# First layer in a written order: scan parts at fixed distances, weight splits in pieces, products in two halves, and changed ends

## The chip, the cores and the metric

The kernel runs on one core of a Trainium2 chip. A core has a matrix engine (TensorE, PE in the profile; its weight loads are shown apart as PEld), a vector engine (VectorE, DVE), a scalar engine (ScalarE, ACT), a general engine (GpSimd, POOL), and an engine that starts transfers (SyncE, SP). Matmuls write to PSUM, which has eight banks of 128 rows by 512 numbers; everything else lies in SBUF. The metric is the device time of one execution in microseconds (us).

## The reference, cut to what matters

The input is x, 512 tokens by 1024 features, float32. There are two layers and a last norm.

```python
# layer 1: Mamba-2 (8 groups g, 4 heads each, head size 64, state 128)
h = rms_norm(x, norm_g)
z, xbc, dt = split(h @ w_in)                  # 2048 gates, 2048 + 2*1024 scan inputs, 32 steps
xs, bm, cm = silu(causal_conv4(xbc))
for each chunk:                               # the kernel takes chunks of 128 tokens
    cb     = cm @ bm.T                        # per group
    y_diag = (cb * decay) @ (xs * dt)         # per head
    y_off  = (cm @ state) * exp(acs)
    state  = state * exp(acs_end) + bm.T @ (xs * dt * to_end)
y = y_diag + y_off + d_skip * xs
u = y * silu(z);  u = u * rsqrt(mean_per_group(u*u) + eps)
x = x + (u * g) @ w_out
# layer 2: differential attention, 8 heads; k, v from rms_norm(x), q and gate from rms_norm(x)
w   = softmax(q1 @ k1.T - alibi) - lam * softmax(q2 @ k2.T - alibi)
x   = x + (rms_norm(w @ v) * silu(gate)) @ w_bo
out = rms_norm(x, final_norm_g)
```

## The kernel before, in words

**Three matmuls for one product.** Dense products keep float32 accuracy by splitting each operand into a head and a rest: head·head, head·rest, rest·head (`mm3`, line 225). These three matmuls of 128x512 are called a step here. Weights come by transfer as `raw` (128 x 2048 numbers a half item); ScalarE makes the heads (`whi`) and VectorE the rests (`wlo`), four operations of 128x512 each for every half item.

**The dense stream.** Layer 1 is a list of items (line 90, `order_a`): `z0 g0 g1 z1 g2 g3 z2 g4 o0 g5 z3 g6 g7 o1 o2 o3`. An item z projects gates of 512 columns for four token tiles, g projects the B, C and two x parts of one group (four banks `pg`), o is a part of the output projection. Each item has two halves of 16 steps. The evictions of a g item are the convolution and SiLU (`xc`), on VectorE and ScalarE, a bank after the other.

**The scan.** `ssd(g)` computes group g from its four `xc` outputs: `pcb` (C by B), `pbt` and `pxt` (transposes of B and of the two x parts), decays times `pcb` (`dec`, on VectorE, from exponentials on ScalarE that `decays` makes for two groups at once), `psA` and `psB` (states), `pyd` (the diagonal part: 16 products of 128x64, in two banks), `po` with `hst` (offsets by the states). Then on VectorE, GpSimd and ScalarE: `tmp` (offsets scaled), sums into `dx`, the gate `zs`, squares, a root by nine small VectorE operations (`rsqrt`, line 231), and the scaling to `tmp` on ScalarE. Last, `pyt` transposes `tmp`, and `yh`, `yl` are the head and rest that the o items read.

**What sets the order.** The program is written against a scheduler that sorts each engine's instructions by its own timeline. A switch per engine (`Ordered`, line 43, `T.on`, `A.on`, `V.on`) keeps an engine in the order of the program instead. Before, all three are off in layer 1 but for the first splits: `ssd(g)` is written when item g has been written, and the scheduler places its parts. In layer 2 TensorE is on for the whole layer: the dense stream is a generator that yields its length after each step, and `paced` lays due pieces of weight splits (`use_b`) beside it. In layer 1 `use` splits whole half items and fetches three half items ahead.

**The end.** The last head's last token tile is turned (`turn`), weighed with the values, normed and gated; beside it runs `rows`, the last output projection, in an order written by hand as (tile, half, heads). A finished half is added to the residual on VectorE (`add`), squared on ScalarE, and its tile's root (`last_root`) scales it on its way out.

Of the kernel before, what the change touches and what calls it, by code (L numbers as in the profile page):

```python
# [17 lines left out]
P = 128  # L18
# [43 lines left out]
def trunk(ctx, tc, x, x_t, par, w_dt, w_in, w_out, w_kvqg, w_bo, d_skip, lam_qk, fin_g, out):  # L62
# [59 lines left out]
    def load(i):  # L122
# [29 lines left out]
        if i == 0:  # L152
# [6 lines left out]
            nc.sync.dma_start(raw[:, 2:4, :].rearrange("p k n -> p (k n)"), src[:, 2 * w:4 * w])  # L159
            for i in range(1, 4):  # L160
                nc.sync.dma_start(xt[i], x_t[:, 2 * i:2 * i + 2, :])
# [15 lines left out]
    def use(seg):  # L177
        fetch(segs.index(seg) + 3)
        return ready.pop(seg)

# [15 lines left out]
    def use_b(seg, first=None, pace=None):  # L196
# [28 lines left out]
    def mm3(ps, lhs, rhs, first, last):  # L225
        (lh, ll), (rh, rl) = lhs, rhs
        T.matmul(ps, lhsT=lh, rhs=rh, start=first, stop=False)
        T.matmul(ps, lhsT=lh, rhs=rl, start=False, stop=False)
        T.matmul(ps, lhsT=ll, rhs=rh, start=False, stop=last)
# [44 lines left out]

    def fill(n):
        for _ in range(n):
            next(dense[0], None)
# [46 lines left out]
    def tok_mm(ps, t, b, w):  # L324
        tk = slice(t * P, (t + 1) * P)
        for k in range(4):
            kk = 4 * b + k
            mm3(ps, (hh[:, kk, tk], hl[:, kk, tk]), (w[0][:, k, :], w[1][:, k, :]), b == 0 and k == 0, b == 1 and k == 3)
            yield
# [27 lines left out]

    first = load(0)()
# [14 lines left out]
    fetch(2)  # L373
    for t in range(NT):
# [73 lines left out]
    ps_tt = ss_bank("ps_tt")  # L448
    for i, src in enumerate((dtp, acs, toe)):
        T.transpose(ps_tt[:, i * P:(i + 1) * P], src, ident)  # L450
    tok = const.tile([P, 4, NQ, H], F32, name="tok")
    V.tensor_copy(tok[:, 0:3].rearrange("p a c h -> p (a c h)"), ps_tt[:, 0:3 * P])
    A.activation(tok[:, 3], tok[:, 1], AF.Exp)
    dt_tok, acs_tok, toe_tok, eacs_tok = (tok[:, i] for i in range(4))

# [24 lines left out]
    def group_proj(g):  # L480
# [3 lines left out]
        for b in range(2):  # L484
            wh, wl = use(("g", g, b))
            for i in range(4):
                cs = slice(i * P, (i + 1) * P)
                for k in range(4):
# [3 lines left out]
                    yield  # L492
# [4 lines left out]
    def out_mm(po, j, t, w):  # L497
        tk = slice(t * P, (t + 1) * P)
        for k in range(4):
            yh, yl = yT[2 * j + k // 2]  # L500
            mm3(po, (yh[:, k % 2, tk], yl[:, k % 2, tk]), (w[0][:, k, :], w[1][:, k, :]), k == 0, k == 3)
            yield

    def out_proj(j):
        for n in range(2 if j < 3 else 1):
            w = (use if j < 3 else use_b)(("o", j, n))
# [9 lines left out]
    def stream_a():  # L516
# [4 lines left out]
        while True:  # L521
            yield

    bss = small.tile([P, 2, NT], F32, name="bss", bufs=1)
    decs = {}

    def decays(j):

        for g in (2 * j, 2 * j + 1):
            hs = slice(R * g, R * g + R)  # L530
            dec = bp.tile([P, R, NQ, P], F32, tag="dec", name=f"dec{g}", bufs=2)
            nc.sync.dma_start(dec.rearrange("p h c l -> p (h c l)"),
                                acs_d[hs].rearrange("h c l -> (h c l)").partition_broadcast(P))
# [13 lines left out]
    def ssd(g):  # L547
        bc, cc, x0, x1 = conv_out.pop(g)
# [4 lines left out]
        pcb = long_bank(f"pcb{g}")  # L553
        for c in range(NQ):
            cs = slice(c * P, (c + 1) * P)
            T.matmul(pcb[:, cs], lhsT=bc[:, cs], rhs=cc[:, cs], start=True, stop=True)
# [4 lines left out]
        A.copy(bt.rearrange("p c n -> p (c n)"), pbt[:, 0:3 * P])  # L561
        xdt = bp.tile([P, NQ, R, HD], F32, tag="xdt", name=f"xdt{g}")
# [15 lines left out]

        hst = bp.tile([P, 3, R, HD], F32, tag="hst", name=f"hst{g}")
# [6 lines left out]
        V.tensor_tensor(out=hsf[:, 1], in0=psA[:, 256:512], in1=hsf[:, 1], op=ALU.add)  # L586
        psB = ss_bank(f"psB{g}")
# [6 lines left out]
        pyd = []  # L594
        for q in range(2):
            pyd.append(ss_bank(f"pyd{g}_{q}"))
            for c in (2 * q, 2 * q + 1):
                for h in range(R):
                    o = (c % 2) * 256 + h * HD
                    T.matmul(pyd[q][:, o:o + HD], lhsT=dec[:, h, c, :], rhs=xdt[:, c, h, :], start=True, stop=True)  # L600
            dq = dx[:, 2 * q:2 * q + 2].rearrange("p c h e -> p c (h e)")
            V.tensor_tensor(out=dq, in0=pyd[q].rearrange("p (c e) -> p c e", c=2), in1=dq, op=ALU.add)
        if g % 2 and g < G - 1:
            decays((g + 1) // 2)

        po1 = ss_bank(f"po1{g}")
# [19 lines left out]
        for c in range(NQ):  # L626
            A.activation(tm[:, c], u[:, c], AF.Copy, scale=r4[:, c:c + 1])
# [454 lines left out]
```

## Time and profile before

| | |
|---|---|
| median of 3 runs | 739.06 us (738.97 to 739.16) |
| profiled execution | 739.31 us |
| its span in the trace | 737.5 us |
| TensorE busy | 723.7 us, 98% |
| VectorE, ScalarE, GpSimd busy | 532.8, 444.7, 115.7 us |
| layer 1, layer 2, tail after the last matmul | about 0 to 440, 440 to 728.5, 728.5 to 737.5 |

A row of the timeline has start, length, engine, line, operation, output<-inputs, shapes and count; in brackets what its engine waited for before. All operations of the three switched engines pass through one helper, so they show line 53 and are told apart by their tiles. Lengths of matmuls are modelled and overlap; the distance between two starts tells what one costs. Groups of instructions give busy time and the mean length of one.

### The profile page before, as it was taken

Reading aid. Unit: us, or ns where it says so; the run is one execution under the profiler, and the core shown is the slowest. Engines: PE = TensorE matmul, PEld = TensorE weight load, DVE = VectorE, ACT = ScalarE, POOL = GpSimd, SP = SyncE. Lnnn points to the kernel's source line nnn. Section 1 sums busy time; section 2 is a strip of 40 time slices with the busy share of each in tenths; the row PEclk is TensorE's granted clock in tenths of the full one; section 3 lists DMA queues with packets and bytes.
Section 4 is the critical chain, followed back from the end, with each engine's and each line's share of the span. In section 5 each row is a group of like instructions: output and inputs, shape, how many; then the busy total and the mean of one; then the engine's idle time right before and its main releaser. Section 6 shows DMA issues by size and latency. Waiting matters only on the chain.

```text
span 737.5 us, 10321 instructions
## 1 busy us (share of the span) xinstructions
PE 723.7 (98%) x3733; PEld 605.8 (82%) x3733; DVE 532.8 (72%) x1202; ACT 444.7 (60%) x974; POOL 115.7 (16%) x158
## 2 busy tenths in 40 slices
PE   9999999999999999999999999999999999999995
PEld 7788878888887888877888879888988898888874
DVE  5679955799668669469895755657767857785876
ACT  5849672865829356256433258767766766755565
POOL 0108141403233141150110201000000000000002
PEclk9999999999999999999999999999999999999998
DMA  8552313124131223132113220331221131131003
GB/s 315 212 194 95 118 55 115 63 109 172 58 114 61 112 114 115 58 115 101 71 58 114 94 79 8 114 115 58 73 100 57 59 115 58 58 105 68 28 1 114
DMA packets 12626, 70.83 MB, mean 96 GB/s; under 512 B 1696, under 2 KB 2464, under 8 KB 5024
## 3 DMA queue, kind: packets, MB, share of 16 engines
q1 hardware_dynamic: 12432, 70.16, 26.2%
q8 instruction: 29, 0.48, 0.3%
q14 instruction: 21, 0.17, 0.1%
q10 hardware_dynamic: 144, 0.02, 0.0%
HBM read 68.02 MB, written 2.16 MB: 95 GB/s over the span
## 4 chain that ended last, share of the span: by engine, by line
PE 85%; DVE 7%; ACT 5%; issue 1%; DMA 1%; POOL 0%; ACTq 0%; POOLq 0%; SPq 0%
PE pg L53 20%; PE po L53 13%; PE pz L53 10%; PE pt L53 7%; PE pq L53 6%; PE pv L53 6%; PE pk L53 6%; PE pyd L53 4%; PE pb L53 3%; PE sc L53 3%; PE pc L53 2%; DVE wlo L53 2%; ACT L53 1%; ACT whi L53 1%; PE pxt L53 1%
## 5 line engine op out<-in xcount | busy, mean ns | idle before, releaser
L53 DVE SCALAR_TENSOR_TENSOR wlo<-raw,prm,whi 128x512 fp32r<-128x512 f32 (+1 forms) x256 | 151.4, 639 | 50.1 <-ACT whi L53 49.8
L53 ACT ACTIVATE whi<-raw,prm 128x512 fp32r<-128x512 f32 (+1 forms) x256 | 136.8, 606 | 55.9 <-PE pz L53 12.9
L53 PE MATMUL pg<-a_hi,whi 128*128 128x512 f32 x256 | 102.4, 401 | 0.4 <-DVE xc L53 0.4
L53 PE MATMUL pg<-a_hi,wlo 128*128 128x512 f32 x256 | 102.7, 405 | 0.0
L53 PE MATMUL pg<-a_lo,whi 128*128 128x512 f32 x256 | 101.4, 397 | 0.0
L53 DVE SCALAR_TENSOR_TENSOR xc<-pg,prc,xc 128x511 f32<-128x511 f32 (+2 forms) x96 | 70.0, 741 | 4.6 <-ACT xc L53 3.8
L53 PEld LDWEIGHTS pg<-a_hi,whi 128*128 128x128 f32 x256 | 48.2, 188 | 11.4 <-issue 0.8
L53 PEld LDWEIGHTS pg<-a_lo,whi 128*128 128x128 f32 x256 | 48.2, 188 | 10.8
L53 PEld LDWEIGHTS pg<-a_hi,wlo 128*128 128x128 f32 x256 | 48.1, 188 | 10.9
L53 PE MATMUL po<-whi,yh 128*128 128x512 f32 x128 | 51.1, 401 | 0.6 <-ACT yh L53 0.6
L53 PE MATMUL po<-wlo,yh 128*128 128x512 f32 x128 | 51.0, 401 | 0.4 <-DVE wlo L53 0.4
L53 PE MATMUL pz<-wlo,a_hi 128*128 128x512 f32 x128 | 50.5, 401 | 0.0
L53 PE MATMUL po<-whi,yl 128*128 128x512 f32 x128 | 50.0, 397 | 0.0
L53 PE MATMUL pz<-whi,a_lo 128*128 128x512 f32 x128 | 49.9, 399 | 0.0
L53 ACT ACT_TABLE_LOAD x33 | 42.3, 1283 | 12.4 <-DVE xc L53 7.6
L53 PE MATMUL pz<-whi,a_hi 128*128 128x512 f32 x128 | 49.5, 399 | 0.2 <-ACT a_hi L53 0.2
L927 POOL TENSOR_TENSOR ot<-ot,fg 128x512 f32<-128x512 f32 x4 | 5.5, 1402 | 257.9 <-ACT ot L53 257.9
L53 ACT ACTIVATE s<-s,mx 128x128 f32<-128x128 f32 (+3 forms) x64 | 35.5, 557 | 9.5 <-DVE mx L53 9.2
L575 POOL TENSOR_TENSOR xe<-xdt,tok 128x256 f32<-128x256 f32 x24 | 15.4, 670 | 152.7 <-DVE xdt L53 152.7
L53 DVE CUSTOM_DVE_ANT_0 s<-sc,bias 128x128 f32<-128x128 f32 (+3 forms) x64 | 29.3, 487 | 12.3 <-PE sc L53 11.8
L53 PE MATMUL pv<-whi,b_hi 128*128 128x256 f32 x128 | 36.6, 286 | 0.0
L537 POOL TENSOR_TENSOR dec<-dec,tok 128x512 f32<-128x512 f32 x32 | 35.9, 1151 | 0.6
(240 smaller groups left out, 1728.7 us busy)
## 6 DMA issues: line engine op xcount, KB each, us to landing
raw<-in_w_in SPq DMA_DIRECT2D x23, 1024.0 KB, 4.8
raw<-in_w_kvqg SPq DMA_DIRECT2D x16, 1024.0 KB, 4.7
dec<-acs_d SPq DMA_DIRECT2D x8, 1024.0 KB, 5.1
raw<-in_w_out SPq DMA_DIRECT2D x8, 1024.0 KB, 4.7
raw<-in_w_bo SPq DMA_DIRECT2D x4, 1024.0 KB, 4.8
x_tok<-in_x SPq DMA_DIRECT2D x4, 512.0 KB, 10.4
out<-ot SPq DMA_DIRECT2D x8, 256.0 KB, 2.1
xt<-in_x_t SPq DMA_DIRECT2D x3, 512.0 KB, 7.8
```

The costliest lines, as they stand in the source:

```text
L53: i = op(*args, **kw)
L537: GP.tensor_tensor(out=dec[:, h], in0=dec[:, h], in1=acs_tok[:, :, R * g + h].unsqueeze(2).to_broadcast([P, NQ, P]), op=ALU.subtract)
L575: GP.tensor_tensor(out=xe[:, c], in0=xdt[:, c], in1=toe_tok[:, c, hs].unsqueeze(2).to_broadcast([P, R, HD]), op=ALU.mult)
L927: GP.tensor_tensor(out=o, in0=o, in1=f, op=ALU.mult)
```

## The change

It has six parts.

1. TensorE is on (in program order) for all of layer 1. `ssd(g)` becomes a generator that yields the number of dense steps until its next part. With `g` done, `pbt` comes after 4 steps, `pcb` at 5, `pxt` at 9 and 13, `psA` at 19, `psB` at 20, `pyd` at 21 and 25, `po` at 29, `pyt` at 45. VectorE, ScalarE and GpSimd stay with the scheduler.
2. The former `use_b` is used for all items: raw weights are fetched two half items ahead, their splits are written in four pieces beside the steps of the half item before.
3. The transfers of the decay rows are issued group by group behind `pyd` (`decay_rows`), and the rest of `decays` is written behind the norm of the odd groups.
4. Each 128x64 product of `pyd` is written as two of 64x64, for output rows 0 to 63 and 64 to 127.
5. At the start: an operation of ScalarE on the identity matrix comes first; two of the first transfers are split in two; group 0's first raw weights are fetched before the weights of dt; the transposes of dt (`tokens`) are placed at step 14 of g0.
6. At the end: the last tile's weights are combined before its turn (`weigh`); the residual is added into the PSUM bank before the last heads of tiles 2 and 3 (`add_in`), the squares and scalings read the bank (`square_in`, `scale_v`); tile 3's matmuls have another order; one of the last two output transfers starts from ScalarE's queue.

```diff
@@ load, use
+            for k in range(2, 4):
+                nc.sync.dma_start(raw[:, k, :], src[:, k * w:(k + 1) * w])
+                nc.sync.dma_start(xt[1][:, k - 2, :], x_t[:, k, :])
-    def use(seg):
-        fetch(segs.index(seg) + 3)
-        return ready.pop(seg)
-    def use_b(seg, first=None, pace=None):
+    def use(seg, first=None, pace=None):
...
+    begin = small.tile([P, 1], F32, name="begin", bufs=1)
+    A.activation(begin, ident[:, 0:1], AF.Copy)
     first = load(0)()
...
     fetch(2)
+    loaded[2] = load(2)
@@ ssd
+        yield 3
         pbt = ss_bank(f"pbt{g}")
...
+        yield 1
+        pcb = long_bank(f"pcb{g}")
...
         for j in range(2):
+            yield 4
             pxt = ss_bank(f"pxt{g}_{j}")
...
+        yield 6
         hst = bp.tile([P, 3, R, HD], F32, tag="hst", name=f"hst{g}")
...
+        yield 1
         psB = ss_bank(f"psB{g}")
...
         for q in range(2):
-            pyd.append(ss_bank(f"pyd{g}_{q}"))
+            yield (1, 4)[q]
+            pyd = ss_bank(f"pyd{g}_{q}")
             for c in (2 * q, 2 * q + 1):
                 for h in range(R):
                     o = (c % 2) * 256 + h * HD
-                    T.matmul(pyd[q][:, o:o + HD], lhsT=dec[:, h, c, :], rhs=xdt[:, c, h, :], start=True, stop=True)
+                    for r in (slice(0, 64), slice(64, 128)):
+                        T.matmul(pyd[r, o:o + HD], lhsT=dec[:, h, c, r], rhs=xdt[:, c, h, :], start=True, stop=True)
...
-        if g % 2 and g < G - 1:
-            decays((g + 1) // 2)
+        if g + 2 < G:
+            decay_rows(g + 2)
+        yield 4
         po1 = ss_bank(f"po1{g}")
...
             A.activation(tm[:, c], u[:, c], AF.Copy, scale=r4[:, c:c + 1])
+        if g % 2 and g < G - 1:
+            decays((g + 1) // 2)
+        yield 16
...
-    decays(0)
-    dense[0] = stream_a()
-    for g in range(G):
-        until(f"g{g}")
-        ssd(g)
-    until("o3")
+    T.on = True
+    dense[0] = paced(stream_a())
+    beside_it = [[0, tokens()]]
+    for _ in dense[0]:
+        for g in range(G):
+            if g in conv_out and f"g{g}" in done:
+                beside_it.append([1, ssd(g)])
+        for e in list(beside_it):
+            e[0] -= 1
+            while e[0] <= 0:
+                n = next(e[1], None)
...
+                e[0] += n
@@ rows and the end
-                         (2, 1, (4, 5, 6)), (2, 0, (7,)), (2, 1, (7,)), (3, 0, (4, 5, 6)),
-                         (3, 1, (4, 5, 6)), (3, 0, (7,)), (3, 1, (7,))):
+                         (2, 1, (4, 5, 6)), (3, 0, (4, 5)), (2, 0, (7,)), (2, 1, (7,)),
+                         (3, 1, (4, 5)), (3, 0, (6,)), (3, 1, (6,)), (3, 0, (7,)), (3, 1, (7,))):
...
+    def add_in(t, n):
+        seeded.add((t, n))
+        V.tensor_tensor(out=pb[t, n], in0=pb[t, n], in1=half(t, n)[0], op=ALU.add)
+    def square_in(t, n):
+        A.activation(half(t, n)[0], pb[t, n], AF.Square, accum_out=fss[:, t, n:n + 1])
...
     turn(h, 2)
+    weigh(h, 3)
...
-    add(3, 0)
-    add(3, 1)
-    scale_v(2, 1, r2)
-    rest3 = last_root(3)
+    square_in(3, 0)
     y, f, o, dst = half(3, 0)
-    V.tensor_tensor(out=o, in0=y, in1=f, op=ALU.mult)
-    r3 = rest3()
+    V.tensor_tensor(out=o, in0=pb[3, 0], in1=f, op=ALU.mult)
+    square_in(3, 1)
+    r3 = last_root(3)()
     A.activation(o, o, AF.Copy, scale=r3)
-    nc.sync.dma_start(dst, o)
+    nc.scalar.dma_start(dst, o)
     scale_v(3, 1, r3)
```

How the order moves is shown at three places, in rows of the programs' instruction lists. First TensorE in item z1, where `pyt` of group 0 stands, before:

```order
L53 MATMUL pz_2_912<-whi_824,a_hi 128x512
L53 MATMUL pz_2_912<-wlo_825,a_hi 128x512
L53 MATMUL pz_2_912<-whi_824,a_lo 128x512
L53 MATMUL pyt_0_763<-ident,tmp_704 128x128
L53 MATMUL pyt_1_770<-ident,tmp_704 128x128
L53 MATMUL pyt_0_763<-ident,tmp_704 128x128
L53 MATMUL pyt_1_770<-ident,tmp_704 128x128
L53 MATMUL pyt_0_763<-ident,tmp_704 128x128 x2
L53 MATMUL pyt_1_770<-ident,tmp_704 128x128 x2
L53 MATMUL pbt_934<-ident,xc_846 128x128 x3
L53 MATMUL pz_2_912<-whi_824,a_hi 128x512
```

and now:

```order
L53 MATMUL pz_3_909<-whi_733,a_hi 128x512
L53 MATMUL pz_3_909<-wlo_734,a_hi 128x512
L53 MATMUL pz_3_909<-whi_733,a_lo 128x512
L53 MATMUL pyt_0_981<-ident,tmp_761 128x128 x4
L53 MATMUL pyt_1_988<-ident,tmp_761 128x128 x4
L53 MATMUL pxt_1_995<-ident,xc_899 128x128 x4
L53 MATMUL pz_3_909<-whi_733,a_hi 128x512
```

`pyt` moved from the second half of z1 (weights `whi_824`) to the last bank of its first half, bank by bank instead of chunk by chunk, and `pxt` of group 1 (`pxt_1_995`) stands right behind it, where before group 1's `pbt` stood.

Second, VectorE ahead of that place, now (`xc`: convolution of group 1, `dec` its decays, `v` and `y_i` the start of group 0's root):

```order
L53 TENSOR_TENSOR pg_3_635<-pg_3_635,ar_row 128x512
L53 SCALAR_TENSOR_TENSOR wlo_913<-raw_731,prm,whi_912 128x512 x4
L53 TENSOR_TENSOR dx_669<-dx_669,zs_2_402 128x256
L53 SCALAR_TENSOR_TENSOR xc_899<-pg_3_635,prc,xc_899 128x511
L53 TENSOR_TENSOR dx_669<-dx_669,zs_3_416 128x256
L53 TENSOR_TENSOR dec_510<-dec_510,pcb_937 128x512 x4
L53 SCALAR_TENSOR_TENSOR xc_899<-pg_3_635,prc,xc_899 128x510
L53 TENSOR_SCALAR v_870<-ss_760 128x4
L53 TENSOR_TENSOR xdt_942<-pxt_0_958,tok 128x4x128
L53 SCALAR_TENSOR_TENSOR xc_899<-pg_3_635,prc,xc_899 128x509
L53 TENSOR_SCALAR y_i<-v_870 128x4
```

Before, the root of group 0 stood behind the last `xc` and `dec` as well, but group 1's `xdt` came after group 0's `pyt`; now `xdt` stands ahead of the root.

Third, TensorE's end, before:

```order
L53 MATMUL pc_1_6800<-whi_6493,oh_6551 128x512
L53 MATMUL pc_1_6800<-wlo_6494,oh_6551 128x512
L53 MATMUL pc_1_6800<-whi_6493,ol_6552 128x512
L53 MATMUL pc_0_6758<-whi_6330,oh_6627 128x512
L53 MATMUL pc_0_6758<-wlo_6331,oh_6627 128x512
L53 MATMUL pc_0_6758<-whi_6330,ol_6628 128x512
L53 MATMUL pc_1_6800<-whi_6493,oh_6627 128x512
L53 MATMUL pc_1_6800<-wlo_6494,oh_6627 128x512
L53 MATMUL pc_1_6800<-whi_6493,ol_6628 128x512
```

and now:

```order
L53 MATMUL pc_0_6869<-whi_6462,oh_6683 128x512
L53 MATMUL pc_0_6869<-wlo_6463,oh_6683 128x512
L53 MATMUL pc_0_6869<-whi_6462,ol_6684 128x512
L53 MATMUL pc_1_6905<-whi_6625,oh_6683 128x512
L53 MATMUL pc_1_6905<-wlo_6626,oh_6683 128x512
L53 MATMUL pc_1_6905<-whi_6625,ol_6684 128x512
L53 MATMUL pc_0_6869<-whi_6462,oh_6759 128x512
L53 MATMUL pc_0_6869<-wlo_6463,oh_6759 128x512
L53 MATMUL pc_0_6869<-whi_6462,ol_6760 128x512
```

`pc_0` and `pc_1` are the two halves of token tile 3; the heads 6 (`oh_6683`) of both halves now stand directly ahead of the heads 7 (`oh_6759`), where before each half took heads 4 to 6 in a row.

More of the change, by code (lines that the diff above doesn't have):

```diff
@@ L273, in trunk @@
     dense = [None]
-    def fill(n):
-        for _ in range(n):
-            next(dense[0], None)
     def until(key):
```

123 lines of the change are left out of this document (75 added, 48 removed).

## The prediction

> **What bounds the kernel now.** I read the page first: busy time and the chain of waits.
>
> ```profile
> PE 723.7 (98%) x3733; PEld 605.8 (82%) x3733; DVE 532.8 (72%) x1202; ACT 444.7 (60%) x974; POOL 115.7 (16%) x158
> PE 85%; DVE 7%; ACT 5%; issue 1%; DMA 1%; POOL 0%; ACTq 0%; POOLq 0%; SPq 0%
> ```
>
> TensorE (PE) is busy for 98% of 737.5 us, so the change can gain by fewer or cheaper matmuls, by the few holes that are left, or at the two ends. Next comes the view of windows, cut at the stages. Its columns are start:end, length, then busy time of PE, weight loads, VectorE (DVE), ScalarE (ACT) and GpSimd, then the granted clock.
>
> ```profile
> 34.00:106.00 72.00, 71.85 (x342) 58.81 (x340) 58.76 (x105) 47.94 (x73) 27.66 (x35) 1.00 0.33 118
> 106.00:157.00 51.00, 50.67 (x254) 41.72 (x255) 36.40 (x65) 31.51 (x56) 12.42 (x17) 1.00 0.26 98
> 208.00:260.00 52.00, 50.96 (x258) 42.09 (x257) 39.08 (x70) 30.89 (x51) 13.38 (x19) 1.00 0.26 92
> 410.00:440.00 30.00, 29.04 (x137) 22.91 (x137) 19.11 (x43) 9.63 (x27) 3.87 (x5) 1.00 0.29 105
> 465.00:700.00 235.00, 235.00 (x1316) 202.34 (x1316) 166.86 (x492) 155.24 (x436) 0.14 (x1) 1.00 0.22 79
> 728.50:737.50 9.00, 0.42 (x2) 0.00 (x0) 5.14 (x11) 2.35 (x6) 2.31 (x2) 0.78 0.46 175
> 57.00:80.00 23.00, 23.00 (x119) 19.26 (x118) 21.90 (x31) 17.84 (x25) 14.43 (x19) 1.00 0.24 83
> ```
>
> Layer 2, already in written order, has no hole in 235 us. Layer 1 (34 to 440) has few: the four rows of it above miss 0.15, 0.33, 1.04 and 0.96 us. The last row is a stretch of layer 1 in which VectorE is busy 21.9 of 23 us. That is the row to remember: over short stretches the second engine is nearly full too. The last 9 us are a tail without TensorE.
>
> **The holes that go.** They are nearly all waits of the transposes `pyt` for the scaled rows `tmp`:
>
> ```profile
> PEld pyt L53 <- ACT tmp L53: 4.7, 13, 1.1
> 105.22 0.40 PE L53 MATMUL pz<-wlo,a_hi 128*128 128x512 f32 x1
> 105.46 0.39 PE L53 MATMUL pz<-whi,a_lo 128*128 128x512 f32 x1
> 106.26 1.52 PE L53 MATMUL pyt<-ident,tmp 128*128 128x128 f32 x6 [0.41 <-ACT tmp L53]
> ```
>
> Dense matmuls start 0.233 us apart, though each is shown as 0.40 long. So this break costs 0.80 − 0.23 = 0.57, not the 0.41 shown as idle. I found eight such breaks between 34 and 440; the same sum over them gives 4.5 us. One, 0.3, is a wait for weights that the new order need not remove. I take **−4.2**, between −2.9 (the windows' idle) and −6.4 (all weight-load waits).
>
> **Products in halves.** One bank of `pyd` is 8 products of 128x64, at two passes each:
>
> ```profile
> 209.92 1.89 PE L53 MATMUL pyd<-xdt,dec 128*128 128x64 f32 x16
> 209.92 1.75 PEld L53 LDWEIGHTS pyd<-xdt,dec 128*128 128x128 f32 x15
> 211.63 0.48 PE L53 MATMUL pg<-a_hi,whi 128*128 128x512 f32 x1
> ```
>
> The bank takes 211.63 − 209.92 = 1.71 us, 0.107 a pass, and there are 16 banks: 27.4 us. The weight load alone fills this (1.75 for 15), so a pass costs what loading 128 columns costs. The change makes 32 passes with 64 columns each. If a load costs by its columns, 32 × 0.053 is the same 1.71: 0 in all. That is my value, because the rows show the load to be the limit and the columns to be loaded do not change. No row shows a 64-column load, so the bounds are far: halves side by side, half the time, −13.7; each half as dear as a whole, +27.4. The Trainium skill, TensorEngine Tiling (Array Packing), Theoretical Speedup, gives up to 2x for a side of 64 or less, and its Key Properties let tiles load and multiply in parallel but make a change of tiling mode drain the engine; by the first the sum would be lower by the 13.7, by the last a little higher, and no row here shows either.
>
> **New waits.** From now on TensorE takes a fixed place in line for each scan part. A part whose operand is late stops all dense work behind it, where the old order let dense steps go first. So each place is a race between TensorE's distance and the chain on VectorE and ScalarE. A step of three matmuls is 0.70 us.
>
> (a) The longest chain is from `po` (offsets by the states) over gate, squares and root to `pyt`. The old trace shows it for g0, while g1's convolutions run too:
>
> ```profile
> 85.95 1.51 PE L53 MATMUL po<-hst,xc 128*128 128x256 f32 x6
> 87.12 0.58 PE L53 MATMUL pz<-whi,a_hi 128*128 128x512 f32 x1
> ...
> 91.66 2.46 DVE L53 TENSOR_TENSOR dec<-dec,pcb 128x512 f32<-128x512 f32 x4
> 96.49 0.94 DVE L53 TENSOR_TENSOR dx<-dx,zs 128x256 f32<-128x256 f32 x1 [0.98 <-POOL dx L620]
> 100.52 0.17 DVE L53 TENSOR_SCALAR v<-ss 128x4 f32<-128x4 f32 x1 [1.73 <-ACT tmp L53]
> 102.32 0.17 DVE L53 SCALAR_TENSOR_TENSOR y_y<-y_c,y_y 128x4 f32<-128x4 f32 x1
> 105.70 1.29 ACT L53 ACTIVATE tmp<-dx,y_y 128x256 f32<-128x256 f32 x3
> ...
> 228.07 1.05 PE L53 MATMUL pcb<-xc,xc 128*128 128x128 f32 x8
> 228.88 0.48 PE L53 MATMUL po<-whi,yh 128*128 128x512 f32 x1
> ...
> 719.36 0.63 PE L53 MATMUL pt<-ident,s 128*128 128x128 f32 x4 [0.67 <-DVE o_y L53]
> 719.74 0.48 PE L53 MATMUL pc<-whi,oh 128*128 128x512 f32 x1
> ```
>
> The root is ready 16.5 us after `po` starts (102.49 − 85.95), with 2.7 idle, and `pyt` came at 20.3. The change wants it 16 steps behind: 11.2 us plus the parts between (by the gaps between the starts in the rows above: `po` 1.2, `pcb` 0.8, and at 0.38 for four transposes `pxt` 0.4, `pbt` 0.3) = 13.9. In the new order VectorE has between them: two `tmp` (0.93), six `xc` at 0.65, one `pg` 0.61, four `wlo` at 0.66, three gates at 0.33, four `dec` at 0.61, `v` and `xdt` 0.8, nine root operations at 0.20: 14.1 us back to back. Four scales on ScalarE at 0.40 follow before the first bank can be turned whole. That is 15.7 at best, a wait of 1.8; with the groups' mean durations instead (0.74 for `xc`, 0.80 for `wlo`, 0.68 for `dec`) it is 4.3. Behind the waiting `pyt` stand the whole z or o item, and through its late evictions the next splits. It happens after each pair of groups (g0, g2, g6). I take 2.6, nearer the row without gaps, since the wait itself lets VectorE catch up: 3 × 2.6 = **+7.8**.
>
> (b) Where no second group follows, the chain is shorter:
>
> ```profile
> 263.24 1.08 PE L53 MATMUL po<-hst,xc 128*128 128x256 f32 x4
> 270.42 1.71 ACT L53 ACTIVATE tmp<-dx,y_y 128x256 f32<-128x256 f32 x4 [2.08 <-DVE y_y L53]
> 273.56 2.55 ACT L53 ACTIVATE whi<-raw,prm 128x512 fp32r<-128x512 f32 x4
> 100.51 1.28 ACT L53 ACT_TABLE_LOAD   x1
> 101.80 2.01 ACT L53 ACTIVATE dec<-dec 128x1024 f32<-128x1024 f32 x2
> ```
>
> It ended 8.9 us after `po` (272.13 − 263.24). The distance is 11.2 + 1.2 = 12.4. But on ScalarE the new order puts four `whi` (2.55), and the exponentials of the next decays with their table loads (up to 4.6), ahead of the scales: 11.4 to 16.0, a wait of 0 to 3.6. I take 1.2 at four places (g1, g3, g4, g5): **+4.8**.
>
> (c) `pxt` of the last convolution output is now due 13 steps and 1.4 us of parts after the group's last matmul, at 10.5 us.
>
> ```profile
> 227.84 0.39 PE L53 MATMUL pg<-a_hi,wlo 128*128 128x512 f32 x1
> 243.69 0.63 ACT L53 ACTIVATE xc<-xc 128x512 f32<-128x512 f32 x1
> ```
>
> For g4 that output came 16.2 us after it (244.32 − 228.07), 5.7 too late, though nothing called for it sooner. For g0, VectorE was as full as the last window row says. Five places (g0, g2, g4, g5, g6) between 0 and half of 5.7; I take 0.6 each: **+3.0**. In all +15.6, and an own range of +9 to +24.
>
> **The ends.**
>
> ```profile
> 718.30 0.39 PE L53 MATMUL pc<-whi,ol 128*128 128x512 f32 x1
> 728.53 0.39 PE L53 MATMUL pc<-whi,ol 128*128 128x512 f32 x1
> 729.61 1.27 DVE L53 TENSOR_TENSOR x_tok<-pc,x_tok 128x512 f32<-128x512 f32 x2
> 731.70 0.29 ACT L53 ACTIVATE f_s<-fss,fvb 128x1 f32<-128x1 f32 x1
> 734.17 0.39 SPq L933 DMA_DIRECT2D out<-ot  x1
> ```
>
> The early `weigh` removes the wait before `pt`, whose row stands above: 719.36 − 718.30 − 0.23 = 0.83. In the tail the two additions leave, and the squares read PSUM right after the last matmul; the second can be done at about 729.9 where the root now starts at 731.70: −1.8, and the second output leaves on its own queue, 0.4 sooner. VectorE still has the scalings of the other tiles in the way there, so I take −1.9 for both. Against it, the matmuls of tile 3's second half with head 6 now wait for `add_in`, a VectorE operation of the size of those at 729.61 (0.6 each): +0.5. The start gains at most 0.2, for the first split is waiting for its data there, and what is not gained is hidden by the warm-up. Sum **−2.4**, from −0.5 to −3.6. The moved decay transfers lie on SP's queue with over 10 us of cover: 0.
>
> **Sum.** The profiled execution is 739.3, its span 737.5, and 1.8 lies around it; the median of the runs is 739.06, so the profiled one stands 0.2 above and I do not correct for it. 739.3 + 15.6 − 4.2 − 2.4 + 0 = 748.3; **748**, own range 741 to 757.
>
> **Rivals.** *A, halves side by side.* The two halves of a product load and multiply at once, for they fill different columns. For it: the pass is bound by its load, so two loads at once would halve it. Against it: one load port is all that the rows show, never two loads at the same time. 748.3 − 13.7 = 734.6, faster; it decides as long as the new waits stay under 20 us (4.2 + 2.4 + 13.7).
>
> *B, the fixed order is fed.* VectorE and ScalarE reach every place in time, as the window of layer 2 has 235.00 of 235. For it: VectorE is 72% busy over all, and the distances of 13 to 16 steps are near the chains' best times. Against it: the 14.1 + 1.6 against 13.9 above. 739.3 − 4.2 − 2.4 = 732.7, faster. With A as well: 719.
>
> *C, a half costs a whole.* The pass has a floor of 0.107 whatever its columns. For it: nothing shows that the load of a half can hide behind the product of the other half; if it cannot, load and product stand one after the other. Against it: now, with whole loads, they do overlap (15 loads in 1.75 beside 16 passes in 1.89). +27.4: 776.
>
> *D, the clock drops.* A wait that lasts makes the granted clock fall: the last window has 0.78 where TensorE rests, and the first transposes of the program take twice as long as later ones:
>
> ```profile
> 1.47 5.23 PE L53 MATMUL warm<-ident 128*128 128x128 f32 x24 [1.47 <-POOL ident masks.py:199]
> ```
>
> 5.23 / 24 = 0.22 each. If each of the three pair waits came with 5.2 us at half speed, 3 × 2.6 more: 756. It decides only where a wait is longer than any hole shown before, 0.8. The Trainium skill, TensorE: Matmul & The Clock Gate, Part 1, has the clock halved after one idle window of about 3.4 us; by that the 2.6 that I take stays clear of it and the upper 4.3 does not.
>
> **How the numbers follow.** Forecast 0.43; A 0.21; B 0.14; A and B together 0.06; C 0.07; D 0.05; new waits that just cancel the gains 0.04. A measurement of this kernel tells 0.2%, 1.5 us, from no change. Faster: A, B and both, 0.41. Same: 0.06. Slower: the forecast, C and D less a little of the forecast's lower edge, 0.53. Leaving out C and A with B (0.13) and some edges, the range is 727 to 760; the forecast alone has 741 to 757.
>
> **What would show it.** The step on halves: the time from the first `pyd` pass of a bank to the next dense matmul, 1.71 (forecast), 0.86 (A) or 3.4 (C). The step on new waits: idle of TensorE before `pyt` and `pxt` released by ScalarE, 2 to 3 us at z1, z2 and o1 and about 1 at four more places; B shows none, and the windows of layer 1 full. The ends: `pt` without a wait, and 7 us instead of 9 after the last matmul. D: a granted clock under 1.00 between 34 and 440. The forecast is wrong if layer 1's TensorE idle grows by less than 9 us, or if the banks move from 1.7.

## The result: slower by 6.3%

The changed kernel takes 787.0 us (median of 4 runs, 782.8 to 789.4), the kernel before 739.11 in the same comparison: a ratio of 1.0633, interval 1.0600 to 1.0665. The profiled execution took 782.77 us, its span is 781.0. In one experiment below (GpSimd in written order) one execution was disturbed (3949 us); its times are given without it, and no profile of it is read.

From the page of the changed kernel: busy time, TensorE's granted clock in 40 slices of the span (an 8 is a slice below nine tenths), and the chain.

```profile
PE 735.7 (94%) x3989; PEld 603.0 (77%) x3989; DVE 537.9 (69%) x1202; ACT 449.6 (58%) x975; POOL 120.4 (15%) x158
PEclk9999999899899999999999999999999999999999
PE 63%; DVE 21%; ACT 7%; issue 5%; DMA 3%; POOL 0%; SPq 0%; ACTq 0%; POOLq 0%; DVEq 0%
```

TensorE's share of the chain of waits falls from 85% to 63%, and VectorE's rises from 7% to 21%. The work of VectorE and ScalarE has hardly grown (532.8 to 537.9 and 444.7 to 449.6 us); TensorE now waits for it. The view of waits names the main places (in total, times, longest):

```profile
PE pyt L53 <- ACT tmp L53: 19.1, 7, 5.0
PE pz L53 <- DVE y_i L53: 5.8, 2, 3.0
PE pxt L53 <- ACT xc L53: 3.1, 2, 2.1
PE ps_tt L53 <- DVE dtp L53: 2.5, 1, 2.5
PE pcb L53 <- ACT xc L53: 1.8, 1, 1.8
```

By the distance between starts of matmuls, less the 0.23 us that a dense one takes, layer 1 has breaks (those over 0.3 us) of 39.7 us; the same count gives 4.1 in the kernel before. Five windows show what else happened (columns as before; the granted clock is the third number from the end):

```profile
112.00:142.00 30.00, 30.00 (x183) 24.30 (x183) 15.22 (x22) 13.73 (x24) 12.21 (x15) 0.95 0.20 71
142.00:148.00 6.00, 1.01 (x5) 0.36 (x3) 2.84 (x12) 5.25 (x10) 1.69 (x3) 0.80 0.49 175
204.00:211.00 7.00, 3.36 (x9) 1.56 (x7) 4.84 (x16) 6.38 (x9) 0.00 (x0) 0.72 0.14 60
301.00:305.00 4.00, 1.65 (x7) 0.79 (x5) 2.01 (x10) 3.45 (x7) 0.60 (x2) 1.00 0.53 221
305.00:310.00 5.00, 4.93 (x18) 3.84 (x19) 1.29 (x2) 1.94 (x5) 0.00 (x0) 0.66 0.01 3
```

The stretch 142 to 148 is one wait: TensorE is busy 1.0 of 6 us. In the last window TensorE is busy 4.93 of 5 us, but at a granted clock of 0.66: the work behind a wait runs slow. The matmuls there show it directly:

```profile
301.47 0.40 PE L53 MATMUL pg<-a_hi,wlo 128*128 128x512 f32 x1
304.07 1.96 PE L53 MATMUL pyt<-ident,tmp 128*128 128x128 f32 x8 [2.21 <-ACT tmp L53]
...
306.54 0.63 PE L53 MATMUL pg<-a_hi,wlo 128*128 128x512 f32 x1
306.97 0.63 PE L53 MATMUL pg<-a_hi,whi 128*128 128x512 f32 x1
...
309.51 0.40 PE L53 MATMUL pg<-a_hi,whi 128*128 128x512 f32 x1
309.75 0.39 PE L53 MATMUL pg<-a_lo,whi 128*128 128x512 f32 x1
```

Between 306.1 and 309.5 dense matmuls start 0.43 us apart instead of 0.23. In the trace's records of the granted clock it is halved for whole windows of 3.41 us, nine times in layer 1, two of them double: 37.5 us. TensorE works in 33.8 of these and so loses 16.9.

The sum, from 739.3 to 782.8 (43.5): +35.6 breaks, +16.9 half clock, −8.5 products in halves (below), −1.9 tail, +0.5 in layer 2 (matmul starts 450.0 to 728.5 before, 494.9 to 773.9 after), −0.8 start (first dense matmul at 6.10 instead of 6.87). That is 41.8; 1.7 are not assigned. This is the fastest of the four executions; the median lies 4.2 higher.

### The profile page after: what moved, and what is told of

It reads as the page before. It is cut to its first block, busy times and chain, and to the rows that moved or that the text cites. A ratio compares the mean times of both kernels' runs of the same rounds, so it can differ in the third digit from the quotient of the medians.

```text
span 781.0 us, 10873 instructions
## 1 busy us (share of the span) xinstructions
PE 735.7 (94%) x3989; PEld 603.0 (77%) x3989; DVE 537.9 (69%) x1202; ACT 449.6 (58%) x975; POOL 120.4 (15%) x158
## 4 chain that ended last, share of the span: by engine, by line
PE 63%; DVE 21%; ACT 7%; issue 5%; DMA 3%; POOL 0%; SPq 0%; ACTq 0%; POOLq 0%; DVEq 0%
PE po L53 12%; PE pg L53 9%; PE pt L53 7%; DVE xc L53 6%; PE pv L53 6%; PE pq L53 6%; PE pk L53 6%; DVE wlo L53 5%; PE pz L53 5%; PE pb L53 3%; PE sc L53 3%; DVE dec L53 2%; PE pyd L53 2%; PE pyt L53 2%; DVE dx L53 2%
## 5 line engine op out<-in xcount | busy, mean ns | idle before, releaser
L53 DVE SCALAR_TENSOR_TENSOR wlo<-raw,prm,whi 128x512 fp32r<-128x512 f32 (+1 forms) x256 | 156.7, 666 | 59.8 <-ACT whi L53 59.4
L53 PE MATMUL pg<-a_hi,whi 128*128 128x512 f32 x256 | 108.1, 422 | 0.7 <-DVE xc L53 0.7
L53 PE MATMUL pg<-a_lo,whi 128*128 128x512 f32 x256 | 103.5, 404 | 0.0
L53 PEld LDWEIGHTS pg<-a_hi,whi 128*128 128x128 f32 x256 | 50.3, 196 | 13.2 <-DVE xc L53 2.0
L53 PE MATMUL pz<-whi,a_hi 128*128 128x512 f32 x128 | 53.5, 430 | 6.0 <-DVE y_i L53 5.8
L53 PEld LDWEIGHTS pg<-a_lo,whi 128*128 128x128 f32 x256 | 49.8, 195 | 10.7
L53 PE MATMUL po<-whi,yh 128*128 128x512 f32 x128 | 53.3, 417 | 0.0
L53 ACT ACTIVATE tmp<-dx 128x256 f32<-128x256 f32 x32 | 13.3, 414 | 54.0 <-DVE dx L53 53.9
L53 ACT ACTIVATE xc<-pg,prc 128x512 f32<-128x512 f32 x32 | 24.7, 772 | 27.5 <-DVE pg L53 27.5
L53 ACT ACTIVATE xc<-xc 128x512 f32<-128x512 f32 x32 | 20.1, 629 | 31.7 <-DVE xc L53 31.4
```

The lines of the kernel that those rows point to most:

```text
L53: i = op(*args, **kw)
```

## The experiments

Each was compared with the kernel before on the same chip (739.4 to 739.8 us in these). "Layer 1's breaks" are counted as above, and half clock is the loss worked out as above.

**Products alone, in both directions.** First whole products in the changed kernel:

```diff
-                    for r in (slice(0, 64), slice(64, 128)):
-                        T.matmul(pyd[r, o:o + HD], lhsT=dec[:, h, c, r], rhs=xdt[:, c, h, :], start=True, stop=True)
+                    T.matmul(pyd[:, o:o + HD], lhsT=dec[:, h, c, :], rhs=xdt[:, c, h, :], start=True, stop=True)
```

> The changed kernel with pyd as whole products of 128x64 again, all else as changed. Theory (the fixed order's waits are the whole loss and the halves gain beside them): the banks go back to 1.79, 787 + 9.9 = 797 us. Rival (the dearer products lie in time that TensorE waits anyhow, so that halves bring nothing there): 787 to 790.

Measured: 795.05 us, ratio 1.0754 (1.0736 to 1.0772): 8.0 more than the changed kernel, as by the theory, with a gain a little smaller than its 9.9. The order of TensorE is written, so no other matmul changes its place; the waits move a little (1.7 us more breaks and 2.1 more half clock than in the changed kernel's trace). A bank in this run, and one in the changed kernel:

```profile
124.79 0.39 PE L53 MATMUL pz<-whi,a_lo 128*128 128x512 f32 x1
125.02 1.89 PE L53 MATMUL pyd<-xdt,dec 128*128 128x64 f32 x16
126.72 0.48 PE L53 MATMUL pz<-whi,a_hi 128*128 128x512 f32 x1
```

```profile
84.48 0.40 PE L53 MATMUL pg<-a_hi,wlo 128*128 128x512 f32 x1
84.81 1.15 PE L53 MATMUL pyd<-xdt,dec 128*64 128x64 f32 x32
85.89 0.50 PE L53 MATMUL pg<-a_hi,whi 128*128 128x512 f32 x1
```

From the dense matmul ahead to the one behind, less its 0.23, whole products take 1.70 us and halves 1.18: 16 × 0.53 = 8.5 with the digits left out here. From the first pass to the next dense matmul the halves take 1.08 instead of 1.70. Their starts come in pairs: the two halves of a pass start within 0.01 us of each other, a pair every 0.06. But the step into the bank costs 0.33 instead of 0.23, and the last pass 0.151 instead of 0.084 (this part lies inside the 1.08), in all 16 banks: 0.16 each for changing to halves and back. The Trainium skill, TensorEngine Tiling (Array Packing), Key Properties, says that changing the tiling mode drains the engine. The rows fit that, with 0.16 us for the pair of changes; that it is a drain they do not show.

Then the halves alone in the kernel before, the same edit reversed:

> The kernel before with one edit: each 128x64 product of pyd is written as two of 64 output rows. In the changed kernel a bank of 32 such passes takes 1.17 us where the kernel before has 1.79 for 16. Theory (the halves themselves are cheaper): a bank falls to 1.17 here too and the time by 16 x 0.62 = 9.9, to 729 us. Rival (the lower cost in the changed kernel comes only with the fixed order around it): the bank stays near 1.8 and the time at 739.

Measured: 747.77 us, ratio 1.0103 (1.0078 to 1.0129), slower. Neither number came. The banks do fall, as by the theory (with `po` behind, a bank's place takes 2.39 instead of 2.89 us in most groups), but the scheduler drew up another order of layer 1, whose breaks are 14.3 us instead of 4.1 with 5.3 us of half clock: −8.5 + 10.2 + 5.3 = +7.0 against +7.4 in the profiled execution (746.66 − 739.31). The largest break and its cause:

```profile
PE po L53 <- DVE x_tok L53: 6.5, 1, 6.5
...
222.88 5.42 POOL L537 TENSOR_TENSOR dec<-dec,tok 128x512 f32<-128x512 f32 x4
223.16 5.68 DVE L53 SCALAR_TENSOR_TENSOR wlo<-raw,prm,whi 128x512 fp32r<-128x512 f32 x4
...
237.47 1.27 DVE L53 TENSOR_TENSOR x_tok<-po,x_tok 128x512 f32<-128x512 f32 x2
238.20 0.80 PE L53 MATMUL po<-whi,yh 128*128 128x512 f32 x1 [6.55 <-DVE x_tok L53]
```

A `po` bank waits for VectorE to add it to the residual. VectorE comes to it late: four `wlo` beside GpSimd's decay subtractions took 5.68 us, where four take 2.6 alone. That is 3.1 of the 6.55; `dec`, four more `wlo` and `xc` stand ahead of the addition too. That pair of rows is what the following runs look into.

**The end and the start alone.** The end of the changed kernel in the kernel before, and both together:

> The kernel before with the changed end alone (weigh, add_in, square_in, order of tile 3, output from ScalarE's queue). In the changed kernel the tail after the last matmul start is 7.1 us instead of 9.0, the wait of 0.82 before the last turn is gone, and two new waits of 0.6 stand before matmuls of the last projection. Theory (the ends are worth the sum): 739.1 - 1.9 - 0.8 + 1.2 = 737.6 us. Rival (the new waits give it back): 739.

> The kernel before with the changed start (an early ScalarE operation, first transfers in pieces) and the changed end, layer 1 otherwise as before. In the changed kernel the first dense matmul starts 0.76 us earlier (6.10 against 6.87). Theory (start and end gains add up): 737.8 - 0.7 = 737.1 us. Rival (the start is hidden behind the first transfers, or the scheduler's order of layer 1 moves): 737.8 or more.

Measured: 737.76 us, ratio 0.9976 (0.9967 to 0.9986), and 737.16 us, ratio 0.9966 (0.9953 to 0.9978). Both as by the theory. Start and end together make the fastest kernel of this study, 2.6 us below the kernel before; it is the version that is left to take.

**TensorE not held to the written order in layer 1.**

```diff
-    T.on = True
     dense[0] = paced(stream_a())
```

> The changed kernel with one line less: TensorE is not held to the program's order in layer 1, so that the scheduler places the scan parts; halves, pieces of splits, two half items ahead, decay transfers and ends stay. Theory (holding TensorE to the fixed distances makes the waits): the 39.8 us of waits and most of the half clock after them go, 787 - 40 - 17 = about 730 us. Rival (weights or decays come late because of the new split and fetch order): waits stay, over 765 us.

Measured: 744.19 us, ratio 1.0070 (1.0047 to 1.0093): 43 us of the loss go with one line, 14 short of the theory's 730. Breaks fall from 39.7 to 15.0, half clock from 16.9 to 4.2. So the written order makes most of the waits (the new split and fetch order stays in this run); but 15 stay even so, the largest a wait of 5.0 of `po` for a bank at the start of o0.

**Distances and decays.** First pyt later:

```diff
-        yield 16
+        yield 24
         yh = bp2.tile([P, 2, S], F32R, tag="yh", name=f"yh{g}", bufs=4)
```

> The changed kernel with pyt 24 instead of 16 steps behind po (5.6 us more for the chain). Theory (the distance to pyt is too short by 1 to 5 us): the seven waits before pyt, 20.5 us in the changed kernel, go, and with them some 10 us of half clock; the waits at the start of g0 and the two of 3.0 us in z1 and z2 stay: about 757 us. Rival (VectorE as a whole is late, so that a wait only moves to the next place): over 775.

Measured: 768.63 us, ratio 1.0398 (1.0382 to 1.0415), between the two. The waits of `pyt` for `tmp` go (one of 2.0 before a `pyt` stays, released by VectorE's `hst`), but the breaks fall only from 39.7 to 35.0; half clock falls from 16.9 to 9.0. The waits have moved:

```profile
PE pxt L53 <- ACT xc L53: 6.5, 5, 3.3
PE pz L53 <- DVE y_i L53: 5.9, 2, 3.1
PE pg L53 <- DVE xc L53: 4.9, 3, 1.8
PE pcb L53 <- ACT xc L53: 4.3, 4, 1.6
```

Now `pcb` and `pxt` of the next group and the banks of `pg` are early. Then the decays written behind `pyt`, alone and with the longer distance:

```diff
-        if g % 2 and g < G - 1:
-            decays((g + 1) // 2)
         yield 16
...
         yT[g] = (yh, yl)
+        if g % 2 and g < G - 1:
+            decays((g + 1) // 2)
```

> The changed kernel with the preparation of the next two groups' decays written behind pyt instead of behind the norm, distances as changed. In the changed kernel GpSimd's four subtractions of it (4.1 us), and ScalarE's exponentials, stand ahead of the norm of g1, g3 and g5, whose pyt waits 5.2, 3.7 and 3.7 us, while g4, with no decays there, waits 2.4. Theory (decays ahead of the norm make the difference): the three fall to 2.4 or less, 787 - 5 - 4 of half clock = 778 us or less. Rival (the chain is late for another reason): 785 to 789.

> Both: pyt 24 steps behind po, and the decays written behind pyt. Theory (each removes a part of the same waits): no wait before pyt; the waits at the start of g0 (about 7 us with half clock) and the two of 3.0 in z1 and z2 remain: 745 to 757 us, the better of the two edits or below. Rival (the decays, pushed behind, are then late for dec of the next group and pyd waits): over 765.

Measured: 789.94 us (ratio 1.0683, 1.0647 to 1.0720) and 769.39 us (1.0403, 1.0382 to 1.0423): no gain from the edit in either. The numbers are nearer to the rivals, though not for the reason that the second rival gives. The trace says why: the scheduler put GpSimd's subtractions where they were. Writing the work later does not move it while that engine is free. The place in question, g1's `pyt` in the changed kernel, engine by engine:

```profile
129.87 1.46 PE L53 MATMUL po<-hst,xc 128*128 128x256 f32 x6
133.43 0.19 POOL L540 COPY een<-dec 128x8 f32<-128x8 f32 x1 [1.69 <-DMA dec<-acs_d]
133.70 4.07 POOL L542 TENSOR_TENSOR dec<-dec,tok 128x512 f32<-128x512 f32 x4
137.73 2.34 POOL L633 TENSOR_TENSOR dx<-dx,tmp 128x256 f32<-128x256 f32 x2
136.90 4.75 DVE L53 SCALAR_TENSOR_TENSOR wlo<-raw,prm,whi 128x512 fp32r<-128x512 f32 x4 [4.51 <-ACT whi L53]
141.58 1.62 DVE L53 TENSOR_TENSOR dx<-dx,zs 128x256 f32<-128x256 f32 x2
145.56 0.16 DVE L53 SCALAR_TENSOR_TENSOR y_y<-y_c,y_y 128x4 f32<-128x4 f32 x1
145.05 2.00 ACT L53 ACTIVATE dec<-dec 128x1024 f32<-128x1024 f32 x2
146.96 1.29 ACT L53 ACTIVATE tmp<-dx,y_y 128x256 f32<-128x256 f32 x3
147.50 0.88 PE L53 MATMUL pyt<-ident,tmp 128*128 128x128 f32 x2 [4.99 <-ACT tmp L53]
```

The additions of `tmp` into `dx` (L633) were ready from 132 on. They stand behind the copy for the next decays, which waits 1.7 us for its transfer, and behind four subtractions of 4.07: two of them start at 137.73. VectorE's four `wlo` take 4.75 beside GpSimd's work, and the gates that need `dx` follow at 141.58. From `po` to the scales it is 17.1 us (146.96 − 129.87) instead of the 7.2 of g4 before (270.42 − 263.24).

**GpSimd's part.** Two ways to test it: hold GpSimd to the written order too, with the decays behind `pyt` as above, or leave its decay work out.

```diff
-    V, A, T = (Ordered(tc, e) for e in (nc.vector, nc.scalar, nc.tensor))
-    GP = nc.gpsimd
+    V, A, T, GP = (Ordered(tc, e) for e in (nc.vector, nc.scalar, nc.tensor, nc.gpsimd))
...
-    T.on = True
+    T.on = GP.on = True
```

> The changed kernel with GpSimd too held to the written order in layer 1, and the decays of the next groups written behind pyt. In the changed kernel the scheduler puts GpSimd's four decay subtractions (4.1 to 4.7 us) between the additions that the norm of g1, g3, g4 and g5 needs, and VectorE's four wlo beside them take 4.8 to 5.4 us instead of 2.6. Theory (GpSimd's order makes the chain late): the four waits before pyt (5.2, 3.7, 2.4, 3.7 = 14.9 us) fall below 1 each and the half clock behind them goes, to 760 to 770 us. Rival (VectorE and ScalarE are late by themselves): over 780 us.

> As the run with GpSimd in written order, and pyt 24 instead of 16 steps behind po. Theory (order and distance are two parts of one lateness): no wait before pyt; what stays is the start of g0 (about 7 us), banks of z1 and z2 that are freed late (2 x 3.0) and some half clock: 745 to 755 us. Rival (the longer distance only moves the waits to pcb, pxt and pyd, as it did with the scheduler's GpSimd order at 768.6): 762 to 769.

> The changed kernel with GpSimd's decay work left out (the subtractions and the causal selection; the decays are then the exponentials of the raw rows, so the output is not the reference's). Everything else, distances too, as changed. Theory (GpSimd's decay work, by its place in the queue and by slowing VectorE beside it, is the larger cause of the waits): VectorE's wlo and gates run at 0.66 and 0.33 us everywhere, the waits of 39.8 us fall by half or more, and the time to 750 to 765 us. Rival (the distances are too short for VectorE and ScalarE alone): over 775.

Measured: GpSimd in written order, 769.2 to 773.7 us, at the theory's upper end, ratio 1.0423 (1.0399 to 1.0448); the same with `pyt` at 24 steps, 759.19 us, ratio 1.0261 (1.0245 to 1.0277), between theory and rival; the decay work left out, 756.54 us, ratio 1.0235 (1.0202 to 1.0268), within the theory's range.

So at the same distance of 16 the order of GpSimd is worth 16 us, and leaving its decay work out 30. The second takes the decay work out of the queue altogether, so that it no longer slows VectorE or holds ScalarE's exponentials; how the 30 divide among these the runs do not show. In the run without the decay work TensorE's waits are halved (breaks 39.7 to 19.1). Before `pyt` of g1, g3, g4 and g5 they are 0.9, 1.2, none and 0.6 instead of 5.15, 3.70, 2.37 and 3.70; the longest that stays is g6's, 2.8 in the view:

```profile
PE pyt L53 <- ACT tmp L53: 6.8, 6, 2.8
PE ps_tt L53 <- DVE dtp L53: 2.6, 1, 2.6
PE pxt L53 <- ACT xc L53: 2.1, 1, 2.1
```

**All parts later.** To the run with GpSimd in order and 24 steps:

```diff
-        yield 14
+        yield 20
         ps_tt = ss_bank("ps_tt")
...
-        yield 1
+        yield 4
         pcb = long_bank(f"pcb{g}")
...
-            yield 4
+            yield (4, 6)[j]
             pxt = ss_bank(f"pxt{g}_{j}")
...
-        yield 6
+        yield 5
         hst = bp.tile([P, 3, R, HD], F32, tag="hst", name=f"hst{g}")
```

> As the run with GpSimd in written order and pyt 24 steps behind po, and with all earlier parts later too: the transposes of dt at step 20 of g0 instead of 14, pcb 3 steps later, pxt 3 and 5 steps later, so that no part is due before its operand by the lags seen (pcb and pxt were 1.0 to 3.4 us early). Theory (what is left is distances alone): the waits before ps_tt, pcb and pxt, 15 us there, go, 759 - 15 - 4 = 740 us. Rival (VectorE has not the time in pairs of groups, so that banks are freed late wherever the parts stand): 750 to 760.

Measured: 748.43 us, ratio 1.0117 (1.0102 to 1.0132), nearer to the rival. No wait is left before `ps_tt` or `pcb`, but 20.1 us of breaks remain, and two thirds of them, the two groups shown, are of another kind:

```profile
PE pg L53 <- DVE xc L53: 11.3, 6, 2.4
PE po L53 <- DVE xc L53: 2.4, 1, 2.4
```

These are the dense stream's own banks: a new item needs a bank whose convolution VectorE has not finished. With the dense items in a fixed order there is nothing else to run there.

**The clock.** Thirty transposes of the identity matrix, thrown away, in front of `pyt` of g1, g3 and g5, where TensorE waits anyway:

```diff
             pyt = ss_bank(f"pyt{g}_{j}")
+            if j == 0 and g in (1, 3, 5):
+                for _ in range(30):
+                    T.transpose(pyt[:, 0:P], ident, ident)
```

> The changed kernel with 30 transposes of the identity matrix (3.3 us at full clock, thrown away) in front of pyt of g1, g3 and g5, where TensorE waits 5.2, 3.7 and 3.7 us anyway. Theory (a wait also halves the clock for 3.4 or 6.8 us behind it): the half windows behind these three waits go, about 6 us less than the changed kernel, 781 us. Rival (only the wait counts): no gain, 787 or a little more.

Measured: 784.88 us (778.5 to 788.0), ratio 1.0601 (1.0551 to 1.0652). Against the changed kernel's 1.0600 to 1.0665 the gain of 2 us isn't clear of the scatter. The trace is clearer. At g3's `pyt`, in the changed kernel and in this run:

```profile
240.00:255.00 15.00, 11.46 (x46) 8.70 (x46) 7.26 (x19) 10.05 (x18) 0.87 (x2) 0.89 0.21 73
```

```profile
244.74 3.44 PE L53 MATMUL pyt<-ident 128*128 128x128 f32 x30
248.44 0.73 PE L53 MATMUL pyt<-ident,tmp 128*128 128x128 f32 x2 [0.26 <-ACT tmp L53]
...
240.00:255.00 15.00, 14.53 (x80) 11.82 (x80) 9.01 (x20) 9.55 (x17) 4.62 (x5) 1.00 0.20 71
```

The granted clock over these 15 us is 1.00 instead of 0.89, and likewise at g5; at g1, where 2.7 of the 5.2 us stay idle, one half window stays instead of two. In all the half-clock time falls from 37.5 to 30.7 us. So it is the idleness of TensorE that halves the clock; its exact price in time is not settled by this run.

The traces of the other runs say how much idleness it takes. The clock's records change only at points that lie whole multiples of 3.41 us apart. Cut the traces of the two kernels and of all runs but GpSimd in written order at these points, from 30 us to 700. Among the windows at full clock in which TensorE idles for 0.5 us or more by the lengths of its rows, a halved window follows all 52 with at least 1.9 us of idleness and none of the 100 with less than 1.3. Of the 39 in between it follows 11; what decides there is open.

**Two more combinations.** TensorE free with GpSimd in written order, the kernel before with start, end and halves, and that with GpSimd in written order:

> The changed kernel with TensorE free in layer 1 again (744.2 us so), and GpSimd held to the written order with the decays behind pyt. Theory (GpSimd's decay work is what the scheduler misjudges, and it is behind the 15 us of waits that were left with TensorE free): waits fall to 5 us or less, 744 - 10 = 734 us. Rival (those waits come from banks and splits, not from GpSimd): 742 to 746.

> The kernel before with start, ends and halves. Halves alone in it gave 747.8, because the scheduler drew up another order with 14.3 us of waits, one of 6.7. Theory (that order was an accident of small changes): here the waits can be near 4 again, 737.2 - 8.6 = 728.6 us. Rival (with cheaper pyd the scheduler's order has such waits by its rules): 743 to 747.

> The kernel before with start, ends and halves, GpSimd in written order from the first decays on, and the decays behind pyt. Theory (GpSimd's decay work ahead of norms is what the scheduler misjudges): waits of layer 1 at 5 us or less, 729 us. Rival (scheduler's order fails elsewhere): over 737.

Measured: 740.67 us (ratio 1.0012, 1.0003 to 1.0021), 742.97 us (1.0055, 1.0037 to 1.0073) and 742.04 us (1.0033, 1.0021 to 1.0046). The first lies between theory and rival, the second at the lower edge of its rival's range, the third within its rival's. All have the gain of the halves, and all have 13 to 14 us of breaks, with one of 3 to 6.5 at the start of o0 behind g4. So the loss with halves under the scheduler is not one unlucky order: it came in every order that it drew up here. GpSimd's order helps in the first (744.2 to 740.7) and does not account for the rest; why the scheduler draws up such orders with halves is open.

Counted over these runs, 739.3 with −8.5 for halves and −2.6 for start and end, plus the breaks above 4.1 and half clock, gives the profiled execution within 2 us in most: 768.1 against 767.5 (24 steps), 760.5 against 759.9 (GpSimd in order, 24 steps), 749.3 against 749.0 (all later), 741.8 against 741.9 (start, end and halves). It misses by 4 to 6 us in the runs with dummy transposes and without decay work.

## Why the prediction was wrong

The direction was right, and so was the kind of reason: fixed places whose operands come too late. The size was wrong by a factor of five: 48 us instead of 9. Two steps failed: the price of the new waits, most of all in step (b), and the clock, which the sum put at nothing. The halves, priced at nothing too, hid 8.5 us of it.

**New waits (+15.6 forecast).** They are 39.7. The step that failed most is (b): the chain where no second group follows, priced at 1.2 each for g1, g3, g4 and g5. They measured 5.15, 3.70, 2.37 and 3.70, 14.9 instead of 4.8. I added up what ScalarE's queue would put ahead of the scales and kept the 8.9 us of the rest of the chain from the old trace; but GpSimd is in that chain too. I never priced its queue, nor what its work does to VectorE beside it (the old trace had it in its means, `wlo` 0.80 and the gates 0.57, and I read them as scatter). The runs without its decay work (−30) and with it in order (−16) show that GpSimd's decay work makes most of it; without that work the four places measure 2.6 together. Step (a), 2.6 at three places, measured 4.5 and 4.2 (each split between `pyt` and a dense matmul in z1 and z2; by the program that one waits for a bank that a late `xc` held, and the view names `y_i`, the operation right behind this `xc`) and 2.9. Its upper value was worked out wrongly: the three means that it names raise 1.8 to 3.2; it takes the means of the gates and of the other operations as well to come above 4. These means are also lengths that overlap, where the row without gaps counts distances between starts. The wait at a bank of the dense stream was in no term; it is also the last thing that stays when all distances are long enough. Step (c) had 3.0 for five `pxt`; `pxt` measured 1.2 and 2.3, but `ps_tt` and `pcb` of g0, which I had left out, 3.3 and 2.0. The run with 24 steps shows a fault of the method as well: with each place priced alone, a cure of one place (20.5 us of waits before `pyt`) took only 4.7 us off the breaks and 7.9 off the half clock, and moved the rest.

**The clock, rival D at 0.05.** It was part of the outcome, with 16.9 us instead of the 7.8 that I gave it; in the sum it stood at nothing, because I took a wait of 2.6 as clear of it. The rows contradict: half clock came after the waits of 2.0 (at 64.8) and 2.4 (at 301.5), and not after 2.3 (at 271.2). The Trainium skill, TensorE: Matmul & The Clock Gate, Part 1, has the clock halved after an idle window of about 3.4 us. The length of the half windows agrees, 3.41. That TensorE must idle for that long does not: 1.9 us within one window of 3.41 was always enough, and 1.3 to 1.9 sometimes. So what a wait costs depends on how it lies to windows that the kernel does not choose. It also differs between executions of the changed kernel: the mean granted clock is 0.973 in the one of 782.8 us and 0.967 in the one of 789.4, about 5 us of the 6.6 between them by an estimate (span times what is missing from 1).

**Products in halves (0 forecast).** −8.5: neither 0 nor rival A's −13.7, but nearer to A. The mechanism that I chose, a load that costs by its columns with one load at a time, was the wrong term: a bank takes 1.08 us instead of 1.70, a factor of 1.6, and the halves start in pairs, so two halves do share time. The change to halves and back costs 0.16, 0.07 of it inside the 1.08, and 1.18 is left against 1.70.

**Holes that go (−4.2).** The count gives 4.1, and they went: 39.7 − 4.1 is the +35.6 of the sum above, where the forecast has 15.6 − 4.2 = 11.4.

**The ends (−2.4).** −2.65 with start and end alone in the kernel before. The tail after the last matmul start is 7.1 us, 1.9 less as forecast, and the 0.83 before `pt` is gone. Two waits of 0.6 came for the one of 0.5 that I gave, and the start brought more than my 0.2.

**Decay transfers (0).** Not quite: the copy that waited 1.69 us for one held GpSimd's queue in front of the additions for g1. What that alone cost was not measured.

**Rival B** is refuted for this order. **Rival C** fell with the first bank.

## What to carry to other kernels

A written order on one engine turns every late operand into idle time for all that stands behind it, so before it is fixed, each place has to be checked against the whole chain, with every engine in it and with the queue of each, not only the two busiest. The banks of the dense stream are such operands too. And a hole on TensorE costs more than its length, for the clock behind it can be halved for 3.41 us, in two cases here for 6.83.

An edit that is cheaper by itself (the halves, 8.5 us) can lose under a scheduler that draws up a new order; measure it once with the order held, to know what it is worth.

## What the runs showed of the hardware

- VectorE's operations with two inputs in SBUF are slower beside GpSimd's work. In the changed kernel, between 34 and 440 us, `wlo` of 128x512 is 0.75 us long on average where no GpSimd operation overlaps it, and 1.26 where such operations cover at least half of it; the gates `dx<-dx,zs` take 0.42 and 0.72. `xc`, which reads one input from PSUM, is 0.74 either way. Without GpSimd's decay work the mean of all `wlo` falls from 0.87 to 0.75 and that of the gates from 0.61 to 0.51; the row of `wlo` in the changed kernel and in that run (busy, mean ns):

```profile
L53 DVE SCALAR_TENSOR_TENSOR wlo<-raw,prm,whi 128x512 fp32r<-128x512 f32 x104 | 84.7, 871 | 34.2 <-ACT whi L53 34.0
L53 DVE SCALAR_TENSOR_TENSOR wlo<-raw,prm,whi 128x512 fp32r<-128x512 f32 x116 | 80.6, 747 | 31.1 <-ACT whi L53 31.0
```

  The Trainium skill, GPSIMD Engine Reference, Specifications, has GpSimd's SBUF interfaces shared with VectorE, with contention for VectorE operations that have two inputs in SBUF; `wlo` and the gates are such, `xc` is not, and the rows agree.
- The clock is halved in whole windows of 3.41 us, once or twice in a row. A halved window followed every full-clock window with 1.9 us or more of idle TensorE (52 of 52 in these traces) and none with 0.5 to 1.3 (0 of 100).
- Two products for 64 output rows each, alternating between the two halves of the array, take 1.08 us for 32 passes where 16 passes over 128 rows take 1.70, and going into this form and out of it costs 0.16 us (0.07 of it in the 1.08).
